# A two-layer hybrid decoder step: ScalarE in program order from the token-major projections to the indexer's end, and the sample tokens' taps as one product and one sum

## The chip, the cores and the metric

The kernel runs on 1 core of a Trainium2 chip. The metric is the device time of one execution in microseconds, the median of several runs.

## The reference, cut to what matters

One inference step over `DEPTH = 2` layers for 1040 prompt tokens (16 meta tokens and 1024) and 64 sample tokens (8 sequences of 8), 1104 columns in all, in float32. Each layer has three branches on one normalised input: a gated linear recurrence, a Conformer convolution and sparse attention whose keys an indexer picks. What the change touches is the gate and the depthwise convolution of the second branch and the projections and scores of the third:

```python
def conformer_conv(glu_in, z, buf, conv_w, conv_b, ln_g, ln_b, conv_pw, w_pb):
    a, g = jnp.split(glu_in, 2, axis=-1)
    u = a * jax.nn.sigmoid(g)
    xp = jnp.concatenate([buf.astype(u.dtype), u], axis=1)
    y = lax.conv_general_dilated(xp, conv_w[:, None, :].astype(xp.dtype), window_strides=(1,), padding='VALID', dimension_numbers=('NWC', 'WIO', 'NWC'), feature_group_count=B_WIDTH) + conv_b
...
def index_scores(qi, wi, ki):
    s = jnp.einsum('bqhd,bsd->bqhs', qi.astype(F32), ki.astype(F32))
    return jnp.einsum('bqhs,bqh->bqs', jax.nn.relu(s), wi.astype(F32) * IDX_SCALE)
```

The convolution has 31 taps and 512 channels (four blocks `c` of 128), the indexer 4 heads of 64.

## The kernel before, in words

**The filler.** The main projections are products of 128 output channels with all 1104 columns. A chunk of 128 channels is worked in three groups of 384, 384 and 336 columns, each 24 matmuls into one PSUM bank `mm` (`stream`, L391): high and low halves of the operands stand apart, so three products make one float32 product. Behind a group's last matmul ScalarE evicts the bank with the bias into `sp` (L204, called behind L391), and behind the third group it issues the DMA that stores the chunk to DRAM (L404). The weights of a chunk are one load `wr`, a cast `wh` on ScalarE in two pieces of 128x512 (L269) and the rest `wl` on GpSimd (L270); the load of the next chunk is asked for ahead of a chunk's first group. This stream is doled out in steps of three matmuls: `fill(key)` takes as many steps as the table `FILL` has under the key, so TensorE always has matmuls between the steps of other work. TensorE's order is the program's order everywhere (`manual_schedule` for that engine); the other engines' orders are a scheduler's, but for VectorE, which keeps program order from the convolution to the masks (the stack `dve`).

**The side work.** The convolution `conv` runs on VectorE: for each of four channel blocks 31 taps over the prompt's 1040 columns (L1492, L1495) and 31 over the 64 sample columns (L1493, L1496). The input `up`, `us` is the projection `ga` times the sigmoid of `gg`; both come back from DRAM, and the sigmoid is one ScalarE operation of 128x1104 for each block (`cy<-cy`). `Side` doles the taps out: each place of the program adds a budget from the table `SIDE` (in ns), each tap pair takes 1420 of it.

**The stretch around the change.** In each layer, one after the other: (1) the first chunks, with budgets `t0`; (2) `cproj`, the token-major projections, two column groups of nine token blocks: weights `cr` are loaded and split into `ch` (ScalarE) and `cl` (GpSimd), each block takes 24 matmuls (L679 to L681) into a bank of `mm` or `tp`, ScalarE copies it to `CTr` (L684), GpSimd adds the bias, and in the second group VectorE rotates it (L722) and takes budget `tr`; (3) `fill("ic")`; (4) `indexer`. It casts the index keys (L733), takes the rest on GpSimd (L734), transposes them (L739) and copies them to `KIH`, `KIL` (L743, L744). Then come the blocks i = 7 to 2 with four heads each: the scores of one head go to the one buffer `lg` (L770, L771; 128(i+1) columns), `fill("is", 7 - i)` takes 6, 4, 7, 6, 7 and 7 steps for i = 7 to 2, ScalarE evicts `lg` through a relu to `rl` (L204, two buffers), and VectorE takes budget `ti` and adds `rl` times a weight to the scores `SC` (L805). The sample tokens' keys (`kir`, `kib`, L888, L893) follow.

Since there is one `lg`, the first score matmul of a head waits until the `rl` of the head before it is done:

```python
for h in range(4):
    ps = lgt()
    ...
    fill("is", 7 - i)
    rl = xt.tile([128, 1152], F32, name="rl", tag="rl")
    act_(rl[:, 0:n], ps[:, 0:n], AF.Relu)
    taps("ti", 7 - i)
```

Of the kernel before, what the change touches and what calls it, by code (L numbers as in the profile page):

```python
# [11 lines left out]
def _quiet(msg, *args, **kwargs):  # L12
# [5 lines left out]
F32 = mybir.dt.float32  # L18
# [31 lines left out]
SIDE = {"t0": (5000, 10000, 10000, 10000, 9300, 10000), "tr": (4200, 4200, 4200, 4200, 4200, 4200, 4200, 2000, 0),  # L50
# [3 lines left out]
KSEL = 4  # L54
# [100 lines left out]
def trunk(tc, a, o, depth=DEPTH):  # L155
# [47 lines left out]
    def act_(out, in_, fn, **kw):  # L203
        S.activation(out, in_, fn, **kw)  # L204
# [136 lines left out]
    def stream(l, pv, chunks, groups, slot, early, lead, more):  # L341


        n = len(chunks)
        blocks = chunks + [("early", (c, bi)) for c in range(8) for bi in range(2)]
        parts = [(c, g) for g in range(3) for c in range(lead)]
        parts += [(i, g) for i in range(lead, n - 2) for g in range(3)]
        parts += [(i, g) for g in range(3) for i in (n - 2, n - 1)]
        parts += [(i, g) for i in range(n, n + 16) for g in range(3)]
        ws, bufs = {}, {}  # L350

        def get(i):
            if i < len(blocks) and i not in ws:
                nm, c = blocks[i]
                if nm == "early":
                    ws[i] = ws[i - 2][1:] if c[0] % 2 else wpair(l, BLK["pb" if c[1] else "pa"] + c[0] // 2)
                else:
                    ws[i] = wchunk(l, BLK[nm] + c, V if i == lead else G, more if 1 < i < lead else None)

        get(0)  # L360
        get(1)
        yield True
        for i, g in parts:
            if g == 0 and 0 < i < lead - 1:
                get(i + 1)
            if lead <= i < n - 1 or i >= n or (i in (lead - 1, n - 1) and g == 2):
                get(i + 1)
            nm, c = blocks[i]
            if nm == "early":
                yield from early.part(c[1], c[0], g, ws[i][0], slot[0])  # L370
                continue
            bcol = BCOL[nm]
            wh, wl = ws[i]
            if g == 0:
                bufs[i] = spt(more if 1 < i < lead else None)
            n0, nn = groups(nm)[g]
            ps = slot[0]()[:, 0:nn]
            sl = slice(n0, n0 + nn)
            H, L = ([x[:, k, sl] for k in range(8)] for x in (XH, XL))
            if i == 0:  # L380

                ops = []
                for k in range(10):
                    if k < 8:
                        ops += [(wh(k), H[k]), (wl(k), H[k])]
                    if k > 1:
                        ops.append((wh(k - 2), L[k - 2]))
            else:
                ops = [(wh(k), x[k]) for k in range(8) for x in (H, L)] + [(wl(k), H[k]) for k in range(8)]
            for j, (w, x) in enumerate(ops):  # L390
                T.matmul(ps, w, x, start=(j == 0), stop=(j == 23))  # L391
                if j == 23:

                    fn = AF.Sigmoid if nm == "gate" and c < 16 else AF.Identity
                    act_(bufs[i][:, sl], ps, fn, bias=pv[:, bcol + c:bcol + c + 1])
                    if nm in ("cz",):

                        if g == 0:
                            sg = spt()
                        act_(sg[:, sl], ps, AF.Sigmoid, bias=pv[:, bcol + c:bcol + c + 1])  # L400
                        G.tensor_tensor(bufs[i][:, sl], bufs[i][:, sl], sg[:, sl], op=OP.mult)
                    if g == 2:
                        lo = groups(nm)[0][0]
                        S.dma_start(fD[nm][c, :, lo:NT], bufs[i][:, lo:NT])  # L404
                    if i == n - 1:
                        early.load(g)
                if j % 3 == 2:
                    yield True
# [164 lines left out]
    def layer(l, hst, late):  # L573
# [39 lines left out]
        slot[0] = mmt  # L613
        ctp = ctr.enter_context(tc.tile_pool(name="ctr", bufs=1, side="right"))
        CTr = ctp.tile([128, 9, 580], F32, name="CTr", tag="CTr")
        cproj(l, CTr, taps)
        scp = scs.enter_context(tc.tile_pool(name="scp", bufs=1))
        SC = scp.tile([128, SCN], F32, name="SC", tag="SC")
        SC8 = scp.tile([128, NT], F32, name="SC8", tag="SC8")
        fill("ic")  # L620
        indexer(l, CTr, SC, SC8, fill, taps)
        ctr.close()
        tk1 = tks.enter_context(tc.tile_pool(name="tk1", bufs=1))
        steps, F = topk(SC, SC8, tk1)
# [30 lines left out]
        return merge(l, pv, late_groups, fill, ers)  # L655


    def cproj(l, CTr, taps):
        with tc.tile_pool(name="cpk", bufs=CPK, side="right") as cpk, tc.tile_pool(name="cpr", bufs=2, side="right") as cpr, \
                tc.tile_pool(name="cpt", bufs=2, side="right") as cpt:  # L660
            for gi, (c0, w) in enumerate(CGROUPS):
                brep = cpr.tile([128, 290], F32, name="brep", tag="brep")
                Y.dma_start(brep[:, 0:w], a["b_in"][l, c0:c0 + w].partition_broadcast(128))
                ch, cl = [], []
                for k2 in range(4):
                    cr = cpr.tile([128, 2, 290], F32, name="cr", tag="cr")
                    Y.dma_start(cr[:, :, 0:w], a["wc"][l, gi, k2])
                    for k in range(2):
                        h_ = cpk.tile([128, 290], F32R, name="ch", tag="ch")
                        l_ = cpk.tile([128, 290], F32R, name="cl", tag="cl")  # L670
                        S.copy(h_[:, 0:w], cr[:, k, 0:w])
                        G.tensor_tensor(l_[:, 0:w], cr[:, k, 0:w], f(h_[:, 0:w]), op=OP.subtract)
                        ch.append(h_)
                        cl.append(l_)
                for t in range(9):
                    rows, ts = TROWS[t], slice(128 * t, 128 * t + TROWS[t])
                    ps = dmt()
                    for k in range(8):
                        T.matmul(ps[0:rows, 0:w], XH[:, k, ts], ch[k][:, 0:w], start=(k == 0), stop=False)  # L679
                        T.matmul(ps[0:rows, 0:w], XH[:, k, ts], cl[k][:, 0:w], start=False, stop=False)  # L680
                        T.matmul(ps[0:rows, 0:w], XL[:, k, ts], ch[k][:, 0:w], start=False, stop=(k == 7))  # L681
                    d0 = c0 - O_C - 512
                    dst = CTr[0:rows, t, d0:d0 + w]
                    S.copy(dst, ps[0:rows, 0:w])  # L684
                    G.tensor_tensor(dst, dst, brep[0:rows, 0:w], op=OP.add)
                    if gi == 1:
                        rope(CTr[0:rows, t, 0:576].rearrange("p (h d) -> p h d", d=64), 9, t, rows, cpt, ((0, 2), (4, 9)))
                        taps("tr", t)
            for dst, j0, j1 in ((kvD.rearrange("t p c -> (t p) c"), 0, 256), (o["kv"][l], 0, 256), (o["ki"][l], 512, 576)):
                Y.dma_start(dst[0:1024].rearrange("(t p) c -> p t c", p=128), CTr[:, 0:8, j0:j1])  # L690
                Y.dma_start(dst[1024:NT], CTr[0:80, 8, j0:j1])
# [772 lines left out]
    def conv(l, pv, cw, c1):  # L1464
        def gated(c):
# [7 lines left out]
            Y.dma_start(y, fD["gg"][c])  # L1473
            Y.dma_start(sr[:, 0], a["state_conv"][l, c])
            G.tensor_copy(us[:, :, 0:30], sr[:, 0])
            act_(y, y, AF.Sigmoid)
            G.tensor_tensor(up[:, 30:1070], up[:, 30:1070], y[:, 0:1040], op=OP.mult)
            G.tensor_tensor(us[:, :, 30:38], us[:, :, 30:38], y[:, 1040:1104].rearrange("p (b q) -> p b q", q=8), op=OP.mult)

# [6 lines left out]
        for c in range(4):  # L1486
            up, us, y = nxt
            yp, ys = y[:, 0:1040], y[:, 1040:1104].rearrange("p (b q) -> p b q", q=8)
            for j in range(31):
                w = cw[:, j, c:c + 1]  # L1490
                if j == 0:
                    V.tensor_scalar(yp, up[:, 0:1040], w, pv[:, 64 + c:65 + c], op0=OP.mult, op1=OP.add)  # L1492
                    V.tensor_scalar(ys, us[:, :, 0:8], w, pv[:, 64 + c:65 + c], op0=OP.mult, op1=OP.add)  # L1493
                else:
                    V.scalar_tensor_tensor(yp, up[:, j:j + 1040], w, yp, op0=OP.mult, op1=OP.add)  # L1495
                    V.scalar_tensor_tensor(ys, us[:, :, j:j + 8], w, ys, op0=OP.mult, op1=OP.add)  # L1496
                if j == 30:
                    Y.dma_start(yD[c], y)
                if j == 14 and c < 3:
                    nxt = gated(c + 1)  # L1500
                yield 1420

    def conv_norm(pv, cn, fill, side):

# [271 lines left out]
```

## Time and profile before

| what | value |
|---|---|
| time, median of 3 runs | 2926.06 us (2922.28 to 2927.58) |
| the profiled execution | 2926.8 us, its span 2924.9 us |
| PE busy | 2757.9 us, 94% of the span |
| DVE busy | 2113.7 us, 72% |
| ACT busy | 1186.8 us, 41% |
| POOL busy | 1247.6 us, 43% |
| chain that ended last | PE 17%, DVE 4%, all others 1% or less |

PE (TensorE) is busy nearly throughout, so the other engines (DVE is VectorE, ACT ScalarE, POOL GpSimd, SP SyncE) matter where PE waits for them. Shares over the whole span hide stages: what a place is worth is read from the waits in its stretch.

### The profile page before, as it was taken

To read this page: it belongs to the slowest core of one execution; us is meant where nothing else is said; L and a number is where in the kernel's file an instruction comes from. 1 tells how busy PE (TensorE), PEld (TensorE's weight loads), DVE (VectorE), ACT (ScalarE), POOL (GpSimd) and SP (SyncE) were. 2 spreads that over 40 slices of the span, in tenths; PEclk is the share of its full clock that TensorE was granted. 3 is DMA by queue.
4 is the path that set the end of the run, shared out by engine and by line. 5 is a ranking of instruction groups with operands and counts; after the bars stand their busy time and mean duration, and the time that the engine had idled before them with its cause. 6 is when DMAs were issued, how large, how long until landed. Compare 5 with 4: busy or idle time off the path is not lost. (4 is left out here: it accounts for less than half of the span.)

```text
span 2924.9 us, 44993 instructions
## 1 busy us (share of the span) xinstructions
PE 2757.9 (94%) x17094; PEld 2620.9 (90%) x17094; DVE 2113.7 (72%) x3832; ACT 1186.8 (41%) x2369; POOL 1247.6 (43%) x978
## 2 busy tenths in 40 slices
PE   7989899999998999999999998998999999999898
PEld 7988879999998888879999997898999989988798
DVE  5798867889969667535366896788899786774443
ACT  4314443323333556544341334422332335565432
POOL 3533334434425214756564332443434241157563
PEclk9999999999999999999999999999999999999999
DMA  4523234332335124666453322323332441247554
GB/s 146 162 61 109 90 103 140 122 112 89 118 130 170 67 67 154 195 201 197 150 169 105 98 83 90 127 99 109 130 112 77 157 151 63 86 150 222 190 166 148
DMA packets 192569, 374.14 MB, mean 128 GB/s; under 512 B 30657, under 2 KB 129697, under 8 KB 192289
## 3 DMA queue, kind: packets, MB, share of 16 engines
q1 hardware_dynamic: 166016, 272.21, 29.7%
q10 hardware_dynamic: 20448, 78.09, 6.6%
q0 software_dynamic: 5888, 20.97, 2.3%
q8 instruction: 134, 2.20, 0.3%
q14 instruction: 83, 0.67, 0.1%
HBM read 251.07 MB, written 122.40 MB: 128 GB/s over the span
## 5 line engine op out<-in xcount | busy, mean ns | idle before, releaser
L391 PE MATMUL mm<-xh,wh 128*128 128x384 f32 (+2 forms) x2656 | 888.1, 336 | 27.6 <-ACT sp L204 23.9
L391 PE MATMUL mm<-xl,wh 128*128 128x384 f32 (+2 forms) x2656 | 886.0, 336 | 0.0
L270 POOL TENSOR_TENSOR wl<-wr,wh 128x512 fp32r<-128x512 f32 x332 | 473.1, 1443 | 697.8 <-ACT wh L269 465.8
L391 PEld LDWEIGHTS mm<-xh,wh 128*128 128x128 f32 x2656 | 506.0, 191 | 41.5 <-ACT sp L204 29.0
L391 PE MATMUL mm<-xh,wl 128*128 128x384 f32 (+2 forms) x2656 | 531.3, 336 | 0.0
L391 PEld LDWEIGHTS mm<-xl,wh 128*128 128x128 f32 x2656 | 506.2, 191 | 7.2 <-issue 1.9
L391 PEld LDWEIGHTS mm<-xh,wl 128*128 128x128 f32 x2656 | 461.8, 192 | 6.3 <-issue 1.9
L916 DVE TENSOR_SCALAR_CACHE_REDUCE jk<-SC,F 80x1104 bf16<-80x1104 f32 (+6 forms) x448 | 448.8, 1002 | 8.4
L204 ACT ACTIVATE sp<-mm,vec 128x384 f32<-128x384 f32 (+1 forms) x356 | 198.6, 564 | 512.0 <-PE mm L391 494.8
L1495 DVE SCALAR_TENSOR_TENSOR cy<-up,vec,cy 128x1040 f32<-128x1040 f32 x240 | 337.9, 1408 | 0.4
L269 ACT CAST wh<-wr 128x512 fp32r<-128x512 f32 x352 | 203.6, 618 | 164.1 <-PE mm L391 80.4
L204 ACT ACTIVATE P<-P,nm 128x896 f32<-128x896 f32 (+7 forms) x128 | 99.5, 778 | 64.1 <-DVE nm L1021 61.7
L1037 DVE TENSOR_TENSOR pl<-tp,ph 128x512 fp32r<-128x512 f32 x144 | 97.8, 687 | 36.9 <-ACT ph L1036 36.1
L1496 DVE SCALAR_TENSOR_TENSOR cy<-us,vec,cy 128x64 f32<-128x64 f32 x240 | 117.2, 488 | 0.0
L1036 ACT CAST ph<-tp 128x512 fp32r<-128x512 f32 x144 | 83.2, 584 | 54.4 <-PE tp L1033 50.2
L1021 DVE CUSTOM_DVE_ANT_0 P<-sc,MB 128x512 f32<-128x512 f32 (+1 forms) x96 | 63.9, 667 | 57.1 <-PE sc L1015 56.2
L1346 PEld LDWEIGHTS lg<-hQ,hK 128*128 128x128 f32 x512 | 65.8, 205 | 28.0 <-issue 19.9
L1025 DVE TENSOR_SCALAR P<-P,nm 128x896 f32<-128x896 f32 (+7 forms) x128 | 87.4, 683 | 4.3
L1346 PE MATMUL lg<-hQ,hK 128*128 128x64 f32 x512 | 66.4, 286 | 25.5 <-DVE hQ L1375 25.3
L1033 PE MATMUL tp<-ident,P 128*128 128x128 f32 x576 | 88.0, 275 | 1.5 <-DVE P L1025 1.5
L204 ACT ACTIVATE rl<-lg 128x1024 f32<-128x1024 f32 (+6 forms) x54 | 42.6, 788 | 102.8 <-DVE SC L805 60.2
L287 PE MATMUL tp<-xh,wh 128*128 128x384 f32 (+2 forms) x240 | 79.9, 335 | 0.4 <-DVE z L1681 0.4
(454 smaller groups left out, 5932.0 us busy)
## 6 DMA issues: line engine op xcount, KB each, us to landing
wr<-in_wp SPq DMA_DIRECT2D x180, 512.0 KB
eg<-gateD SPq DMA_DIRECT2D x80, 184.0 KB
gateD<-sp ACTq DMA_DIRECT2D x24, 552.0 KB
gateD<-sp ACTq DMA_DIRECT2D x24, 544.0 KB
cr<-in_wc SPq DMA_DIRECT2D x16, 290.0 KB
gt<-gateD SPq DMA_DIRECT2D x24, 192.0 KB
za<-zaD SPq DMA_DIRECT2D x24, 192.0 KB
ggD<-sp ACTq DMA_DIRECT2D x8, 552.0 KB
```

The lines of the kernel that those rows point to most:

```text
L204: S.activation(out, in_, fn, **kw)
L269: S.copy(wh[:, k:k + 4], wr[:, k:k + 4])
L270: (eng or G).tensor_tensor(wl[:, k:k + 4], wr[:, k:k + 4], f(wh[:, k:k + 4]), op=OP.subtract)
L391: T.matmul(ps, w, x, start=(j == 0), stop=(j == 23))
L916: V.tensor_scalar(jk[0:rows, 0:n], s, F.bitcast(F32)[0:rows, j:j + 1], None, op0=OP.is_ge, op1=OP.add, accum_out=cnt[0:rows, j:j + 1])
L1025: V.tensor_scalar(p[:, 0:n], p[:, 0:n], nm[:, 3:4], None, op0=OP.mult)
L1033: T.transpose(ps[:, 128 * c:128 * c + 128], P[c][:, 128 * kt:128 * kt + 128], ident)
L1036: S.copy(ph, ps)
L1037: V.tensor_tensor(pl, ps, f(ph), op=OP.subtract)
L1346: T.matmul(ps[:, 64 * c:64 * c + 64], K[:, 128 * c:128 * c + 128], up(Q[:, 128 * c:128 * c + 128], m), start=True, stop=True)
L1495: V.scalar_tensor_tensor(yp, up[:, j:j + 1040], w, yp, op0=OP.mult, op1=OP.add)
L1496: V.scalar_tensor_tensor(ys, us[:, :, j:j + 8], w, ys, op0=OP.mult, op1=OP.add)
```

## The change

Four edits, the first three of order and of arithmetic, the last of the two budgets:

1. `cproj` first loads and splits the weights of both column groups, then enters ScalarE into program order; `act.close()` ends that behind the indexer. So ScalarE's order there is now the order in which the program is written.
2. The sigmoid of `gg` for blocks c = 2 and 3 is taken in the eviction of the projection; blocks 0 and 1 keep the operation of their own.
3. The 31 sample taps of a block become, four times, one product of 128x496 (two sequences x 8 tokens x 31 taps) and one sum over the taps; then one addition of the bias. The product tile takes the buffer of `sr` (tag `sr`, one buffer). A prompt tap is priced 1200, a product with its sum 1300.
4. `SIDE`: `tr` goes from 4200 to 3200 (2000 to 1000), `ts` from 3000 to 4000.

```diff
-SIDE = {"t0": (5000, 10000, 10000, 10000, 9300, 10000), "tr": (4200, 4200, 4200, 4200, 4200, 4200, 4200, 2000, 0),
-        "tk": 4200, "ti": (1400, 2800, 2800, 2800, 2800, 2800), "ts": 3000,
+SIDE = {"t0": (5000, 10000, 10000, 10000, 9300, 10000), "tr": (3200, 3200, 3200, 3200, 3200, 3200, 3200, 1000, 0),
+        "tk": 4200, "ti": (1400, 2800, 2800, 2800, 2800, 2800), "ts": 4000,
...
-                    fn = AF.Sigmoid if nm == "gate" and c < 16 else AF.Identity
+                    fn = AF.Sigmoid if (nm == "gate" and c < 16) or (nm == "gg" and c >= 2) else AF.Identity
...
-        cproj(l, CTr, taps)
+        act = ExitStack()
+        cproj(l, CTr, taps, act)
...
         indexer(l, CTr, SC, SC8, fill, taps)
+        act.close()
...
+                groups.append((gi, c0, w, brep, ch, cl))
+
+            act.enter_context(tc.manual_schedule(engines={mybir.EngineType.Activation}))
+            for gi, c0, w, brep, ch, cl in groups:
                 for t in range(9):
...
-            act_(y, y, AF.Sigmoid)
+            if c < 2:
+                act_(y, y, AF.Sigmoid)
...
-                    V.tensor_scalar(ys, us[:, :, 0:8], w, pv[:, 64 + c:65 + c], op0=OP.mult, op1=OP.add)
                 else:
                     V.scalar_tensor_tensor(yp, up[:, j:j + 1040], w, yp, op0=OP.mult, op1=OP.add)
-                    V.scalar_tensor_tensor(ys, us[:, :, j:j + 8], w, ys, op0=OP.mult, op1=OP.add)
+                if j < 4:
+
+                    b2 = us[:, 2 * j:2 * j + 2, 0:8]
+                    pr = c1.tile([128, 2, 8, 31], F32, name="spr", tag="sr")
+                    V.tensor_tensor(pr, bass.AP(b2.tensor, b2.offset, [*b2.ap, [1, 31]]),
+                                    cw[:, :, c].unsqueeze(1).unsqueeze(1).to_broadcast([128, 2, 8, 31]), op=OP.mult)
+                    V.tensor_reduce(ys[:, 2 * j:2 * j + 2], pr, AX.X, OP.add)
+                    yield 1300
+                if j == 4:
+                    V.tensor_scalar(ys, ys, pv[:, 64 + c:65 + c], None, op0=OP.add)
...
-                yield 1420
+                yield 1200
```

TensorE's order is the same in both programs, instruction for instruction. ScalarE's is not; three places follow.

ScalarE in layer 0, in `cproj`, the program before: copies of token blocks to `CTr` (blocks 4 and 5 around the sigmoid of channel block 2).

```order
L684 COPY CTr_1210<-tp_1343 128x290
L684 COPY CTr_1210<-tp_1370 128x290
L204 ACTIVATE cy_1665<-cy_1665 128x1104
L684 COPY CTr_1210<-tp_1397 128x290
L684 COPY CTr_1210<-mm_1424 128x290
```

In the changed program the copies (L691 there) stand one behind the other; there is no sigmoid of that kind for blocks 2 and 3.

ScalarE in layer 0, from the last `CTr` copy to the cast of the index keys, before:

```order
L684 COPY CTr_1210<-mm_1879 80x290
L204 ACTIVATE sp_1935<-mm_1936,vec_107 128x384
L204 ACTIVATE sp_1935<-mm_1962,vec_107 128x384
L733 CAST rl_2069<-CTr_1210 128x8x64
L269 CAST wh_2016<-wr_2015 128x512 x2
L204 ACTIVATE sp_1935<-mm_1988,vec_107 128x336
L404 DMA vD_92<-sp_1935 128x1104
L733 CAST rl_2069<-CTr_1210 80x64
```

and in the changed program:

```order
L691 COPY CTr_1195<-mm_1841 80x290
L269 CAST wh_1890<-wr_1889 128x512 x2
L204 ACTIVATE sp_1897<-mm_1898,vec_107 128x384
L204 ACTIVATE sp_1897<-mm_1924,vec_107 128x384
L204 ACTIVATE sp_1897<-mm_1950,vec_107 128x336
L404 DMA vD_92<-sp_1897 128x1104
L269 CAST wh_1978<-wr_1977 128x512 x2
L204 ACTIVATE sp_1985<-mm_1986,vec_107 128x384
L740 CAST rl_2031<-CTr_1195 128x8x64
```

The cast of the keys, which stood ahead of the third group's eviction, now stands behind it, its DMA, the next weights and the next chunk's first eviction.

ScalarE in the indexer of layer 0, the four heads of block 7, before (`rl` reads a head's scores `lg`, `sp` evicts a filler group):

```order
L204 ACTIVATE rl_2227<-lg_2202 128x1024
L204 ACTIVATE sp_2188<-mm_2189,vec_107 128x384
L204 ACTIVATE rl_2264<-lg_2232 128x1024
L762 CAST qs_2240<-tp_2237 64x2x128
L763 CAST qs_2240<-tp_2237 64x2x128
L204 ACTIVATE cy_2496<-cy_2496 128x1104
L204 ACTIVATE sp_2188<-mm_2220,vec_107 128x384
L204 ACTIVATE rl_2293<-lg_2269 128x1024
L269 CAST wh_2312<-wr_2311 128x512 x2
L204 ACTIVATE rl_2333<-lg_2298 128x1024
L204 ACTIVATE sp_2188<-mm_2274,vec_107 128x336
L404 DMA aqD_90<-sp_2188 128x1104
```

and in the changed program, the same heads:

```order
L204 ACTIVATE sp_2146<-mm_2147,vec_107 128x384
L204 ACTIVATE rl_2185<-lg_2160 128x1024
L769 CAST qs_2197<-tp_2194 64x2x128
L770 CAST qs_2197<-tp_2194 64x2x128
L204 ACTIVATE sp_2146<-mm_2178,vec_107 128x384
L204 ACTIVATE rl_2221<-lg_2189 128x1024
L204 ACTIVATE rl_2250<-lg_2226 128x1024
L204 ACTIVATE sp_2146<-mm_2231,vec_107 128x336
L404 DMA aqD_90<-sp_2146 128x1104
L269 CAST wh_2271<-wr_2270 128x512 x2
L204 ACTIVATE rl_2292<-lg_2257 128x1024
```

Where a filler group ends in a head's fill, its `sp` (and behind a 336 group the DMA and mostly the next `wh`) now stands ahead of that head's `rl`; before, `rl` stood ahead of it.

## Rows read from the trace of the kernel before

**Rows 1.** PE, waits in 60:347 us, layer 0: releaser, total, times, longest (us)

```profile
PE tp L679 <- ACT CTr L684: 6.2, 1, 6.2
PE mm L391 <- ACT sp L204: 6.0, 2, 4.3
PE lg L770 <- ACT rl L204: 4.1, 4, 1.6
PE tp L777 <- ACT KIL L744: 1.7, 1, 1.7
PE lg L770 <- DVE qs L764: 0.7, 1, 0.7
```

**Rows 2.** Timeline of ACT, 143:167 us: start, length, instruction, [idle before <-releaser]

```profile
165.09 1.12 ACT L204 ACTIVATE cy<-cy 128x1104 f32<-128x1104 f32 x1 [20.48 <-DMA cy<-ggD]
```

**Rows 3.** Stretches: each engine's busy us (x), granted PE clock, DMA share, GB/s

```profile
166.50:171.10 4.60, 4.54 (x19) 4.54 (x20) 3.88 (x4) 1.19 (x5) 4.54 (x5) 0.51 0.02 3
215.10:219.30 4.20, 4.12 (x18) 4.03 (x18) 4.20 (x6) 0.03 (x1) 3.65 (x3) 0.59 1.03 347
231.60:327.00 95.40, 89.64 (x515) 85.46 (x516) 91.96 (x123) 39.02 (x74) 30.88 (x20) 1.00 0.26 86
1662.00:1666.20 4.20, 4.12 (x19) 4.12 (x20) 4.17 (x7) 2.52 (x6) 1.24 (x2) 0.59 0.49 77
```

**Rows 4.** PE, waits in 1500:1765 us, layer 1; the `lg` row in 60:1765, both layers

```profile
PE mm L391 <- ACT sp L204: 2.1, 2, 1.7
PE mm L679 <- ACT sp L204: 3.2, 1, 3.2
PE tp L777 <- ACT KIL L744: 2.0, 1, 2.0
PE tp L739 <- POOL rl L734: 1.0, 1, 1.0
...
PE lg L770 <- ACT rl L204: 8.2, 8, 1.6
```

**Rows 5.** Timeline of ACT, 231:262 us, the first indexer heads of layer 0

```profile
234.91 0.58 ACT L204 ACTIVATE sp<-mm,vec 128x384 f32<-128x384 f32 x1 [1.06 <-PE mm L391]
...
240.77 0.58 ACT L204 ACTIVATE sp<-mm,vec 128x384 f32<-128x384 f32 x1
241.25 1.02 ACT L204 ACTIVATE rl<-lg 128x1024 f32<-128x1024 f32 x1
243.66 1.14 ACT L269 CAST wh<-wr 128x512 fp32r<-128x512 f32 x2 [1.39 <-PE mm L391]
...
245.87 0.53 ACT L204 ACTIVATE sp<-mm,vec 128x336 f32<-128x336 f32 x1
246.44 0.33 ACTq L404 DMA_DIRECT2D aqD<-sp  x1
...
259.90 0.92 ACT L204 ACTIVATE rl<-lg 128x896 f32<-128x896 f32 x1 [2.47 <-DVE SC L805]
```

**Rows 6.** Timeline of PE, 232:236 and 260.5:262 us, in the same heads

```profile
233.32 1.55 PE L391 MATMUL mm<-xh,wl 128*128 128x384 f32 x8
234.71 0.34 PE L391 MATMUL mm<-xh,wh 128*128 128x384 f32 x1
...
260.87 0.50 PE L770 MATMUL lg<-KIH,qs 128*128 128x512 f32 x1 [1.40 <-ACT rl L204]
261.21 0.39 PE L771 MATMUL lg<-KIL,qs 128*128 128x512 f32 x1
```

**Rows 7.** Groups of 231:327 us by shape: busy us, mean ns, idle before

```profile
L204 ACT ACTIVATE rl<-lg 128x768 f32<-128x768 f32 x4 | 3.2, 812 | 7.8 <-DVE SC L805 5.5 <-DVE SC L803 2.2
...
L204 ACT ACTIVATE rl<-lg 128x384 f32<-128x384 f32 x3 | 1.5, 486 | 6.0 <-DVE SC L805 6.0
```

**Rows 8.** Timeline of POOL, 205:222 us: the split of the index keys in layer 0

```profile
213.73 1.55 POOL L734 TENSOR_TENSOR rl<-CTr,rl 128x512 f32<-128x512 f32 x1 [14.55 <-ACT rl L733]
```

**Rows 9.** The page's groups, whole program: the sample tokens' taps

```profile
L1496 DVE SCALAR_TENSOR_TENSOR cy<-us,vec,cy 128x64 f32<-128x64 f32 x240 | 117.2, 488 | 0.0
```

More of the change, by code (lines that the diff above doesn't have):

```diff
@@ L655, in layer, with cproj @@
         return merge(l, pv, late_groups, fill, ers)
-    def cproj(l, CTr, taps):
+    def cproj(l, CTr, taps, act):
         with tc.tile_pool(name="cpk", bufs=CPK, side="right") as cpk, tc.tile_pool(name="cpr", bufs=2, side="right") as cpr, \
                 tc.tile_pool(name="cpt", bufs=2, side="right") as cpt:
+            groups = []
             for gi, (c0, w) in enumerate(CGROUPS):
```

## The prediction

> **What bounds the kernel now.** The table of engines says it first: PE is busy 94% of the span, so a microsecond is won or lost where PE waits. I therefore read the list of PE's waits, stretch by stretch, and then the engine named as releaser on its own timeline.
>
> In layer 0, from 60 to 347 us, PE waits for ScalarE in four places that the change touches [rows 1]: 6.2 us for a copy to `CTr`, 6.0 in two waits for a filler eviction (4.3 and 1.7), 4.1 in four waits for `rl`, 1.7 for the last key copy; and 0.7 for VectorE's `qs`. The first has a plain cause: ScalarE stood 20.48 us in front of the sigmoid of channel block 2, waiting for its input's DMA, with finished banks queued behind it [rows 2]. Each long wait costs twice, since PE then runs at the lower of its two clocks (1.2 instead of 2.4 GHz) for a while. The granted clock was 0.51 over the 4.6 us behind the 6.2 us wait and 0.59 over the 4.2 us behind the 4.3 us wait [rows 3]: 4.6 x 0.49 = 2.25 and 4.2 x 0.41 = 1.72 us lost. Layer 1 shows the same places with 2.1, 3.2, 2.0 and 1.0 us and for `rl` another 4.1, half of both layers' 8.2 [rows 4], and 0.59 for 4.2 us behind the 2.0 us wait, 1.72 lost [rows 3].
>
> In the indexer's heads PE is busy 89.64 of 95.40 us at clock 1.00 [rows 3]: only 5.8 us could be gained there. VectorE, busy 91.96, is nearly full, yet PE waits just 4.1 us for what VectorE holds up.
>
> **Removed.** The sigmoids of blocks 2 and 3 as operations, hence the 6.2 us and its clock; the eviction queued behind the keys' cast, hence 4.3 and its clock; the eviction wait of 1.7 at the heads' end; all four `rl` waits (they come back below, from another cause); `qs` 0.7; of the key copies' 1.7 all but 0.4, which I leave for the twelve copies themselves. Layer 0: 6.2 + 6.0 + 4.1 + 1.3 + 0.7 = 18.3, plus clocks 2.25 + 1.72 = 4.0, together 22.3 us. Layer 1: 2.1 + 4.1 + 3.2 + 1.6 + 1.0 = 12.0, plus 1.7, together 13.7. Sum 36.0 us.
>
> **Added: a wait in most heads.** PE's order is unchanged, so which filler group ends in which head's fill is fixed and can be counted. In program order `rl` stands behind the eviction of such a group, while the next head's first matmul needs `rl` done. The time from the group's last matmul to that point is a sum of rows. The eviction starts 0.20 us after the matmul that follows the group (234.91 against 234.71) [rows 5, 6]. ScalarE goes on 0.48 us after a 384 eviction starts (240.77 to 241.25), 0.57 after a 336 one; then 0.36 for the chunk's DMA issue (0.33 in the row) and 1.03 for a pair of `wh` (1.14 long, overlapping the next) [rows 5]. `rl` takes 1.02 at 1024 columns [rows 5], 0.92 at 896 [rows 5], 0.81 at 768 and 0.49 at 384 [rows 7]; 640 and 512 lie between, 0.70 and 0.60. PE starts 0.05 after it (259.90 + 0.92 = 260.82 to 260.87) [rows 5, 6]. Against this stands the head's remaining fill: (234.71 - 233.32) / 8 = 0.175 us per matmul of 384 [rows 6], 0.153 at 336.
>
> Worked out, with what is left of the fill in brackets:
> - block 7: head 0, 0.20 + 0.48 + 1.03 + 0.05 - 1.05 (6 matmuls) = 0.71; head 1, nothing left, 1.76; head 3, 336 group with DMA and `wh`, 3.24 - 2.10 = 1.15
> - block 6: heads 0 and 2, nothing left, 1.65 each
> - block 5: 1.44, 0.49, 1.08 and, a 336 group with the DMA but `wh` behind, 0.20 + 0.57 + 0.36 + 0.81 + 0.05 = 1.99
> - block 4: 0.51 and 1.88; block 3: 0.71; block 2: 0.30 and, three matmuls left, 0.20 + 0.57 + 0.36 + 1.03 + 0.49 + 0.05 - 0.52 = 2.18
>
> Fourteen waits, 17.5 us per layer, the same in both. VectorE does not lengthen them: budget `ti` is unchanged and buys less work than before.
>
> **Added elsewhere.** The keys' cast now stands behind the third group's eviction, a `wh` pair and the next eviction. In layer 1 the last of these ends three filler steps before the transposes: 0.20 + 0.48, the cast at about 0.6 (the 384 eviction's length [rows 5]), GpSimd's rest at 1.55 [rows 8], two hand-overs of 0.05, less 9 x 0.175: 1.4 us. In layer 0 VectorE's rotations may be later still: between 1.4 and 4.3, the wait that this place had [rows 1]; I take 2.3, near the low end, as `tr` gives VectorE less to do there. The sample keys' copies stand behind one more `wh` pair: 1.1 per layer [rows 5]. Sum of new waits: 2 x 17.5 + 1.4 + 2.3 + 2 x 1.1 = 40.9 us. A wait also costs its restart, about 0.1 us (the first matmul behind one lasts 0.50, the next 0.39 [rows 6]); there are some 14 more waits than before: 1.4.
>
> **Clock of the new waits.** No drop shows behind the waits of up to 1.6 in the heads (clock 1.00), a drop behind 2.0 [rows 1, 3, 4]. I take a drop behind the two longest of each layer, 1.99 and 2.18, at 1.7 each: 6.8 us; the ends are none and one behind each of the six waits over 1.6 per layer, 20.4 us.
>
> The Trainium skill ("TensorE: Matmul & The Clock Gate", section "A second HAM failure mode: psum-queue depth-cycling") says that frequent short idles between matmul groups can by themselves make the clock swing between its two levels; by that rule the sum would take the upper end, 20.4 in place of 6.8. The trace speaks against it so far: the heads already had short waits at clock 1.00 [rows 3].
>
> **Off the path.** The 240 small taps took 117.2 us of VectorE, 0.488 each [rows 9]. In their place come 32 products, 32 sums and 8 additions; between 0.49 and 1.55 each (the small tap, GpSimd's 512-column operation [rows 8, 9]), 35 to 112 us: VectorE gains 5 to 82 us, I take about 70, as for operations that VectorE does alone. It is worth 0 to PE, whose waits for VectorE here are the 0.7 already counted; it shortens only the lag behind `SC`. Its first product waits for the store that frees the `sr` buffer, ahead of which VectorE merely takes longer for block 0. The second column group's weight splits moved ahead of the first group's copies cost 0 as long as the filler's weights of those chunks are there in time; if not, up to 6.2, the longest wait here [rows 1], which the range includes.
>
> **The sum.** New 40.9 + 1.4 + 6.8 = 49.1, removed 36.0: 13.1 us slower. The profiled execution took 2926.8 (span 2924.9 and 1.9 around it), 0.7 above the median: 2926.8 + 13.1 - 0.7 = 2939.2 us against 2926.1.
>
> **The rivals.** A measurement of this kernel can tell about 0.2% (5.9 us) from no change.
> - *The waits come, the clock holds.* Each head's wait stays below what drops the clock. For it: clock 1.00 behind waits of 1.4 to 1.6 [rows 3, 6]. 2926.1 + 4.9 + 1.4 = 2932.4, at the edge of no change.
> - *The eviction costs a head nothing, so the change is faster.* If the group's eviction lies wholly beside PE's last fill matmuls, each wait loses 0.20 + 0.48 + 0.05 = 0.73: nine long ones lose 6.6 and the five short ones vanish, 2.7, so 18.6 over both layers. 2932.4 - 18.6 = 2913.8. It decides where ScalarE gets to `rl` less than 0.1 us behind the group's end. Against it: the lag of 0.20 and the step of 0.48 are read from rows [rows 5, 6].
> - *The clock drops behind every wait above 1.6.* 2932.4 + 20.4 = 2952.8. For it: they follow one another within 4 to 8 us, closer than before.
> - *It does nothing on balance.* ScalarE's new order gives back as much as it takes, and the products take as long as the small taps: 2926.
>
> **How the numbers follow.** Forecast 0.38, clock holds 0.24 (0.14 of it within 0.2%), eviction hidden 0.20, clock drops everywhere 0.12, nothing 0.06. So faster 0.20, same 0.14 + 0.06 = 0.20, slower 0.38 + 0.10 + 0.12 = 0.60. As both signs hold weight, the range reaches from the hidden-eviction case to the all-drops case, 2913 to 2953; the forecast's own range is 2932 to 2946 (no drop, four more drops).
>
> **What would show it.** In the profile after: no `cy` sigmoid of 20 us idle and no 6.2 us wait in `cproj`; in the heads some 14 waits of `lg` for `rl` with 17 us in each layer, the longest about 2.2 in block 2, with `rl` directly behind `sp` on ScalarE; a granted clock below 1.00 in the heads; VectorE's total down by tens of us. Wrong would be `lg` waits below 9 us per layer (evictions hidden), VectorE as the releaser of them, or a PE wait in the first chunks for weights.

## The result, and the profile after

The changed kernel takes 2950.68 us (median of 4, 2944.35 to 2952.47) beside 2924.86 for the kernel before in the same comparison: ratio 1.0083, 95% interval 1.0068 to 1.0098. It is 25.8 us slower, inside the range of 2913 to 2953, with the sign that was forecast; the forecast's own 13.1 us was half of it, and the time lies outside the forecast's own range of 2932 to 2946.

The span was cut at the first matmuls of three places, all starts read from PE's timeline: `cproj`, the first head, the first transposition of the sample keys (`kir`), in both layers.

| stretch, us | before | after | difference | in the prediction |
|---|---|---|---|---|
| start to `cproj`, layer 0 | 127.8 | 128.6 | +0.8 | 0 |
| `cproj` to the first head, layer 0 | 103.75 | 102.91 | -0.8 | -14.2 |
| heads, layer 0 | 105.63 | 117.38 | +11.8 | +11.7 and 3.4 for the clock |
| `kir` of layer 0 to `cproj` of layer 1 | 1235.3 | 1239.0 | +3.7 | +1.1 |
| `cproj` to the first head, layer 1 | 95.54 | 88.11 | -7.4 | -6.5 |
| heads, layer 1 | 105.55 | 118.98 | +13.4 | +11.7 and 3.4 for the clock |
| the rest | 1151.3 | 1155.8 | +4.5 | +1.1 |

(The prediction's 1.4 us of restarts lie over all rows.) So the heads came as worked out, layer 1 too, and layer 0's stretch ahead of the heads gave nothing.

PE's waits in the changed kernel, 60 to 348 us (layer 0) and then 1570 to 1790 us (layer 1); columns as in [rows 1]:

```profile
PE lg L777 <- ACT rl L204: 15.3, 13, 2.1
PE tp L746 <- POOL rl L741: 14.1, 1, 14.1
```

```profile
PE tp L746 <- POOL rl L741: 1.0, 1, 1.0
PE tp L784 <- ACT KIL L751: 0.4, 1, 0.4
```

All waits of [rows 1] but that for `rl` are gone in layer 0. In their place stand 15.3 us for `rl` in 13 waits, and one of 14.1 us for the index keys' rest on GpSimd (layer 1 shows the same 15.3 and 13, and 1.0). Who is late for that one shows on ScalarE's timeline and on VectorE's:

```profile
203.23 0.58 ACT L204 ACTIVATE sp<-mm,vec 128x384 f32<-128x384 f32 x1 [2.04 <-PE mm L391]
216.52 0.62 ACT L740 CAST rl<-CTr 128x512 fp32r<-128x512 f32 x1 [12.71 <-DVE CTr L729]
```

```profile
175.58 0.79 DVE L725 TENSOR_TENSOR rA<-CTr,cb 128x144 f32<-128x144 f32 x1 [2.93 <-POOL CTr L692]
...
206.81 3.97 DVE L1502 SCALAR_TENSOR_TENSOR cy<-up,vec,cy 128x1040 f32<-128x1040 f32 x3
...
216.09 0.34 DVE L729 TENSOR_TENSOR CTr<-rA,rB 128x32 f32<-128x32 f32 x2
```

ScalarE had evicted the filler's group at 203.23, as the program order says, and then stood 12.71 us for VectorE's rotation of the eighth token block, whose last operation began at 216.09. Behind the cast comes GpSimd's rest, which before began at 213.73 [rows 8]; GpSimd's timeline now:

```profile
217.22 1.55 POOL L741 TENSOR_TENSOR rl<-CTr,rl 128x512 f32<-128x512 f32 x1 [13.86 <-ACT rl L740]
```

So VectorE got there 3.5 us later, not earlier, and TensorE, freed of the waits ahead, arrived at 204.8 (218.82 less 14.06) and waited.

The timelines show two things behind VectorE's lateness. The DMA that ScalarE's sigmoid had waited for [rows 2] now holds up GpSimd's product for `up`, with the bias additions and so the first rotation behind it. And since program order puts the casts `wh` ahead of the keys' cast, GpSimd's two splits `wl` now lie among the rotations (at 189.03 and 200.74 us; before, the first began at 215.25, behind them). Beside them VectorE's pair of operations L729, 0.34 us in most other blocks, lasted 4.17 and 2.47 us. GpSimd's and VectorE's timelines of the changed kernel:

```profile
164.52 2.03 POOL L1485 TENSOR_TENSOR up<-up,cy 128x1040 f32<-128x1040 f32 x1 [5.46 <-DMA cy<-ggD]
```

```profile
187.62 4.17 DVE L729 TENSOR_TENSOR CTr<-rA,rB 128x32 f32<-128x32 f32 x2
```

```profile
189.03 2.55 POOL L270 TENSOR_TENSOR wl<-wr,wh 128x512 fp32r<-128x512 f32 x2
```

The heads, PE's timeline in layer 0: the first head waits after the change, against the list in the prediction (0.71, 1.76, 1.15 in block 7; 1.65 and 1.65 in block 6; 1.44 in block 5):

```profile
236.27 0.50 PE L777 MATMUL lg<-KIH,qs 128*128 128x512 f32 x1 [0.54 <-ACT rl L204]
...
242.44 0.50 PE L777 MATMUL lg<-KIH,qs 128*128 128x512 f32 x1 [1.58 <-ACT rl L204]
...
251.38 0.50 PE L777 MATMUL lg<-KIH,qs 128*128 128x512 f32 x1 [1.01 <-ACT rl L204]
...
256.03 0.50 PE L777 MATMUL lg<-KIH,qs 128*128 128x512 f32 x1 [1.48 <-ACT rl L204]
...
263.81 0.50 PE L777 MATMUL lg<-KIH,qs 128*128 128x512 f32 x1 [1.48 <-ACT rl L204]
...
272.21 0.50 PE L777 MATMUL lg<-KIH,qs 128*128 128x512 f32 x1 [1.35 <-ACT rl L204]
```

Each is 0.1 to 0.2 us shorter than worked out, and at its place. The stretches of the heads show a clock of 1.00 and 0.99 (columns as in [rows 3]; the first row is the 14 us wait, the second what follows it, at 0.52; the last two are what follows the longest wait of the heads, 2.09 us, in layer 0 and in layer 1):

```profile
204.70:218.80 14.10, 0.06 (x1) 0.00 (x0) 13.85 (x24) 0.62 (x1) 1.55 (x1) 0.57 0.11 39
218.80:224.00 5.20, 5.17 (x20) 5.08 (x21) 0.76 (x5) 4.18 (x8) 0.32 (x1) 0.52 0.95 316
231.50:348.88 117.38, 101.94 (x576) 95.35 (x576) 107.33 (x107) 40.97 (x81) 35.99 (x25) 1.00 0.24 85
1675.95:1794.93 118.98, 103.54 (x576) 96.93 (x576) 107.87 (x113) 40.98 (x81) 36.67 (x25) 0.99 0.24 84
338.20:343.00 4.80, 4.72 (x27) 4.72 (x28) 4.67 (x4) 0.42 (x2) 2.04 (x2) 1.00 0.35 117
1782.70:1787.00 4.30, 4.29 (x16) 4.29 (x17) 4.26 (x3) 0.00 (x0) 1.96 (x2) 0.61 0.29 88
```

So the same wait left the clock at 1.00 in layer 0 and was followed by 0.61 over 4.3 us in layer 1: 4.3 x 0.39 = 1.7 us, about the 1.6 us by which layer 1's heads are the longer ones.

### The profile page after: what moved, and what is told of

Read it like the earlier page. It is cut to its first block, busy times and chain, and to the rows that moved or that the text cites. A ratio compares the mean times of both kernels' runs of the same rounds, so it can differ in the third digit from the quotient of the medians.

```text
span 2950.7 us, 44803 instructions
## 1 busy us (share of the span) xinstructions
PE 2759.6 (94%) x17094; PEld 2618.0 (89%) x17094; DVE 2125.1 (72%) x3656; ACT 1185.2 (40%) x2365; POOL 1257.7 (43%) x978
## 5 line engine op out<-in xcount | busy, mean ns | idle before, releaser
L1502 DVE SCALAR_TENSOR_TENSOR cy<-up,vec,cy 128x1040 f32<-128x1040 f32 x240 | 356.1, 1484 | 5.8
L287 PE MATMUL tp<-xl,wh 128*128 128x384 f32 (+2 forms) x240 | 78.7, 330 | 0.0
L1040 PEld LDWEIGHTS tp<-ident,P 128*128 128x128 f32 x576 | 70.2, 140 | 7.0 <-DVE P L1032 1.9
```

Of the source, the lines that this page charges most:

```text
L287: T.matmul(ps[:, 0:nn], wk, x, start=(n == 0), stop=(n == 3 * K - 1))
L1040: T.transpose(ps[:, 128 * c:128 * c + 128], P[c][:, 128 * kt:128 * kt + 128], ident)
```

## The experiments

All twelve, with the stretches of their profiled executions (ahead of the heads in layer 0, heads, ahead of the heads in layer 1, heads; us). The ratio is to the kernel before in the same comparison; it need not be the quotient of the two medians.

| run | median us | ratio (95%) | layer 0 ahead | heads | layer 1 ahead | heads |
|---|---|---|---|---|---|---|
| before | 2924.9 | 1 | 103.8 | 105.6 | 95.5 | 105.6 |
| the change | 2950.7 | 1.0083 (1.0068, 1.0098) | 102.9 | 117.4 | 88.1 | 119.0 |
| e1_rl_first | 2925.8 | 1.0007 (0.9994, 1.0020) | 102.5 | 106.3 | 88.1 | 106.3 |
| e2_tr_low | 2965.7 | 1.0148 (1.0127, 1.0169) | 89.2 | 117.6 | 89.2 | 120.6 |
| e4_sched_order | 2938.1 | 1.0043 (1.0023, 1.0064) | 108.3 | 111.9 | 91.1 | 111.8 |
| e5_sigmoid_only | 2917.0 | 0.9984 (0.9970, 0.9997) | 104.4 | 105.6 | 92.1 | 104.4 |
| e6_products_only | 2943.1 | 1.0070 (1.0044, 1.0096) | 109.9 | 109.2 | 99.9 | 108.2 |
| e7_rl_first_taps_later | 2915.4 | 0.9969 (0.9958, 0.9981) | 89.2 | 106.4 | 89.2 | 106.5 |
| e8_split_only | 2925.9 | 1.0006 (0.9992, 1.0020) | 104.5 | 105.6 | 99.2 | 105.7 |
| e9_sigmoid_taps_later | 2916.7 | 0.9976 (0.9961, 0.9991) | 102.8 | 106.5 | 90.9 | 106.5 |
| e10_small_taps_best | 2904.3 | 0.9926 (0.9911, 0.9941) | 92.7 | 102.6 | 88.1 | 101.7 |
| e11_products_old_price | 2934.8 | 1.0028 (1.0013, 1.0043) | 111.8 | 109.7 | 96.5 | 108.8 |
| e12_close_early | 2916.3 | 0.9964 (0.9952, 0.9975) | 89.2 | 110.7 | 89.2 | 110.9 |
| e13_no_edit3 | 2951.1 | 1.0087 (1.0061, 1.0114) | 102.4 | 117.3 | 92.7 | 117.3 |

**The heads: `rl` ahead of the filler.**

```diff
-                    fill("is", 7 - i)
                     rl = xt.tile([128, 1152], F32, name="rl", tag="rl")
                     act_(rl[:, 0:n], ps[:, 0:n], AF.Relu)
+                    fill("is", 7 - i)
```

> The changed kernel with one edit: in the indexer's heads the relu `rl` is written ahead of the filler call instead of behind it; TensorE's order is the same. Theory A (the eviction that stands ahead of `rl` makes the heads' waits): the waits of `lg` for `rl`, 30.6 us in 26 over both layers in the changed kernel, fall to about the 8 us of before, and the time by 20 to 24 us, to about 2928. Theory B (VectorE sets the pace of the heads through the two `rl` buffers): the waits stay above 20 us with VectorE's `SC` as what ScalarE waits for, and the time moves by less than 8 us.

2925.8 us: two lines exchanged took back 24.9 us by the medians, 22 by the ratios. The heads fell from 117.4 and 119.0 to 106.3, their waits in layer 0 from 15.3 to 4.9 us. PE's waits in 60 to 338 us of this run, and the longest of what ScalarE waits for in 231 to 337 us, in the heads, first of this run, then of the change:

```profile
PE tp L746 <- POOL rl L741: 13.9, 1, 13.9
PE lg L777 <- ACT rl L204: 4.9, 3, 2.3
```

```profile
ACT rl L204 <- DVE SC L812: 25.9, 11, 4.7
```

```profile
ACT sp L204 <- PE mm L391: 52.1, 17, 4.3
```

With `rl` behind the filler ScalarE stood 52 us for the filler's matmuls in front of `sp`, with a finished `lg` queued behind; with `rl` first it waits for VectorE's `SC` instead, as before the change [rows 7]. Theory A. The 13.9 us wait for the keys stayed and cost nothing against before, since the whole stretch is as long as before (102.5 against 103.8).

**Layer 0 ahead of the heads: who is late.** Three runs bear on it. The first gives VectorE fewer taps between the rotations:

```diff
-SIDE = {"t0": (5000, 10000, 10000, 10000, 9300, 10000), "tr": (3200, 3200, 3200, 3200, 3200, 3200, 3200, 1000, 0),
+SIDE = {"t0": (5000, 10000, 10000, 10000, 9300, 10000), "tr": (1200, 1200, 1200, 1200, 1200, 1200, 1200, 0, 0),
...
```

> The changed kernel with the budget `tr` at 1200 instead of 3200 for each token block (0 instead of 1000 for the eighth): 12 prompt taps of 1.3 us, some 15 us of VectorE, move from between layer 0's rotations to places behind. Theory A (VectorE's chain of rotations and taps sets layer 0's 14.1 us wait for the index keys): the wait falls to 3 us or less, the clock behind it stays at 1.00, and the time falls by 10 to 14 us, to about 2938. Theory B (ScalarE's new order or GpSimd's bias additions set it): the wait stays above 10 us and the time stays. Theory C (the taps moved are late for the convolution's norm): the wait falls but the time stays within 5 us, with a new wait of PE behind the heads.

PE's waits, 60 to 260 and then 345 to 480 us of this run:

```profile
PE tp L746 <- POOL rl L741: 1.0, 1, 1.0
```

```profile
PE tp L1532 <- POOL nsq L1529: 13.6, 1, 13.6
```

The wait for the keys fell from 14.1 to 1.0 and the stretch from 102.9 to 89.2: VectorE's rotations and taps set it, theory A for the place. The time rose by 15 us, for theory C's reason but by more than its 5: the taps moved were left over behind the indexer and came back as 13.6 us at the convolution's norm in each layer. Layer 1, where nothing was to gain, lost them whole.

The second puts the sigmoid alone into the kernel before (edit 2):

> The kernel before with edit 2 alone: the sigmoid of blocks 2 and 3 in the projection's eviction. Theory A (VectorE's chain of rotations is the bound of layer 0's stretch, and the 6.2 us wait for the copy only lay ahead of it): the 6.2 us wait and the 20.5 us of ScalarE go, a wait for the eviction or for the index keys takes their place, the first head of layer 0 starts within 2 us of 231.6, and the time falls by 2 to 6 us (layer 1's 3.2 us and little more), to about 2921. Theory B (each removed wait is gain, as the prediction had it): the first head of layer 0 starts 8 us earlier, the time falls by 11 us or more, to 2914 or less.

2917.0 us, 7.1 us faster by the medians and 4.7 by the ratio (0.9 to 8.8): nearer to theory A. The 6.2 us wait is gone, and this stands in its place (PE's waits, 60 to 260 us, and ScalarE's timeline there):

```profile
PE mm L391 <- ACT sp L204: 13.4, 1, 13.4
```

```profile
210.23 0.62 ACT L733 CAST rl<-CTr 128x512 fp32r<-128x512 f32 x1 [18.48 <-DVE CTr L722]
...
217.01 0.24 ACT L733 CAST rl<-CTr 80x64 fp32r<-80x64 f32 x1 [4.68 <-DVE CTr L722]
```

The 13.4 us are longer than the 6.2 and 4.3 of before together; ScalarE's cast of the keys, which the scheduler put ahead of the eviction, waits for VectorE. The stretch is 104.4 us long, 103.8 before: taking the sigmoid's wait away gave layer 0 nothing. What the run gained lies in layer 1 (4.6 us in its two stretches) and outside the stretches of the table.

The third does both, in the kernel before: the sigmoid in the eviction, `tr` 2800 in place of 4200, `ts` 4500 in place of 3000.

> The kernel before with the sigmoid in the eviction and some 8 tap pairs moved out of layer 0's and 1's rotations: `tr` 2800 in place of 4200 (1400 for the eighth), `ts` 4500 in place of 3000. Theory A (behind the 6.2 us wait stood VectorE's chain): the 13.4 us wait for the eviction that the sigmoid alone leaves falls to 3 us or less, time 2903 to 2909. Theory B (something else holds the keys' cast, GpSimd or ScalarE's order): the wait stays above 8 us, time 2915 or more.

2916.7 us and a wait of 14.1 us for `sp`: theory B. VectorE was done with the eighth block's rotation at 204.5 there, but the scheduler had put both casts of the keys ahead of two filler evictions, and the second waits for the ninth block. So the two halves need each other: program order for ScalarE, and a shorter chain on VectorE.

**Both, with the moved taps where VectorE stands idle.** The change with `rl` first, `tr` 1200, and `ts` 6000:

> The changed kernel with `rl` ahead of the filler, `tr` at 1200 and `ts` raised from 4000 to 6000, so that the 12 taps moved out of the rotations run where VectorE stood idle for 14.9 and 11.9 us (its waits for the sample scores). Theory A (VectorE's chain makes the 14 us wait of layer 0, and the 13.6 us wait at the convolution's norm came from taps left over behind the indexer): both waits go, time 2910 to 2916, below both kernels. Theory B (the taps moved cost wherever they stand): a wait of over 8 us at the norm stays, time 2925 or more.

2915.4 us, 8.3 below the kernel before, theory A. Both waits are gone (keys 1.0 us, norm 3.7 as in the kernel before), and layer 0's stretch takes 89.2 us as layer 1's does.

**The products.** Edit 3 alone in the kernel before:

> The kernel before with edit 3 alone: products and sums for the sample taps with their prices 1300 and 1200; the budgets, ScalarE's order and the sigmoid are those of before. Theory A (VectorE's share is off TensorE's path, as the prediction had it): VectorE busy 50 to 90 us less, time within 6 us of 2924. Theory B (the cheaper prices put more taps of 1.3 us into each budget, 2800 / 1200 in place of 2800 / 1420, and so make the rotations and the heads later): VectorE's total falls by less than 30 us, layer 0's rotations end some 8 us later and the heads wait more for `rl`, time 2935 to 2945.

2943.1 us, theory B: 19 us slower, all four stretches longer (by 6.1, 3.6, 4.3 and 2.7). VectorE's busy time went from 2113.7 to 2110.7 us, in the change to 2125.1. The groups of the changed kernel, and two places where VectorE works alone, first before, then after:

```profile
L1502 DVE SCALAR_TENSOR_TENSOR cy<-up,vec,cy 128x1040 f32<-128x1040 f32 x240 | 356.1, 1484 | 5.8
L1507 DVE TENSOR_TENSOR spr<-us,vec 128x496 f32<-128x496 f32 x32 | 46.1, 1441 | 5.5 <-DMA out_s_conv<-sr 5.5
L1509 DVE TENSOR_REDUCE cy<-spr 128x16 f32<-128x496 f32 x32 | 21.5, 671 | 1.1
```

```profile
140.22 1.29 DVE L1495 SCALAR_TENSOR_TENSOR cy<-up,vec,cy 128x1040 f32<-128x1040 f32 x1
141.43 0.28 DVE L1496 SCALAR_TENSOR_TENSOR cy<-us,vec,cy 128x64 f32<-128x64 f32 x1
141.62 1.29 DVE L1495 SCALAR_TENSOR_TENSOR cy<-up,vec,cy 128x1040 f32<-128x1040 f32 x1
```

```profile
206.81 3.97 DVE L1502 SCALAR_TENSOR_TENSOR cy<-up,vec,cy 128x1040 f32<-128x1040 f32 x3
```

A tap pair goes by in 141.62 - 140.22 = 1.40 us although its halves last 1.29 and 0.28. Taps one behind another, each reading what the one ahead wrote, follow at (3.97 - 1.29) / 2 = 1.34. So where VectorE is alone a small tap costs 0.06 us, 2 us a block, and not the 0.488 of [rows 9]. What replaced it, in the changed kernel where VectorE is alone too:

```profile
161.88 1.29 DVE L1502 SCALAR_TENSOR_TENSOR cy<-up,vec,cy 128x1040 f32<-128x1040 f32 x1
163.09 1.05 DVE L1507 TENSOR_TENSOR spr<-us,vec 128x496 f32<-128x496 f32 x1
164.18 0.67 DVE L1509 TENSOR_REDUCE cy<-spr 128x16 f32<-128x496 f32 x1
164.77 2.87 DVE L1502 SCALAR_TENSOR_TENSOR cy<-up,vec,cy 128x1040 f32<-128x1040 f32 x1
```

A product with its sum costs 164.77 - 161.88 - 1.34 = 1.55 us there, 6.2 a block. These are prices for VectorE alone; over the whole program its busy time moved by only -3.0 us (this run) and +11.4 (the change), so the gain of about 70 is not there, and no loss of 4 us a block either. And a tap of 1.34 us was now priced 1200 where a pair of 1.40 had been priced 1420, so each budget held more time than before. The same run with the old price, its edit against this one:

```diff
-                    yield 1300
+                    yield 0
...
-                yield 1200
+                yield 1420
```

> The kernel before with edit 3 alone, as in the run that gave 2943.1, but a prompt tap priced 1420 as a pair was and a product with its sum 0, so that each place takes the taps that it took before. Theory A (the price of 1200 for a tap of 1.34 us made the run 19 us slower, more taps in each place): layer 0's wait for the keys falls from 18.2 to near what the kernel before shows, layer 1's 6.0 to near 1, time 2924 to 2932. Theory B (the products and sums themselves do it): the waits stay within 4 us of 18.2 and 6.0, time 2938 or more.

2934.8 us, between the theories: of the 19 us some 11 went with the price (ratios 1.0070 and 1.0028) and 8 stayed with the products. Layer 1's wait of 6.0 us went; in layer 0 a wait of 14.2 us for `sp` took the place of the 18.2 for the keys. Its profiled execution took 2949.3, so its stretches are above its median; that split is a rough one. And the change with edits 3 and 4 undone:

> The changed kernel with edits 3 and 4 undone: small sample taps, their price of 1420 and the budgets of before; ScalarE's program order, the split loops and the sigmoid in the eviction stay, and `rl` stays behind the filler. Theory A (the heads' waits make the loss, the products add to it through VectorE): the waits for `rl` stay near 30 us over both layers, layer 0's wait for the keys is 8 to 14 us, time 2936 to 2944, some 10 us below the changed kernel. Theory B (the products cost nothing in this setting, since layer 0's rotations are late either way): within 4 us of 2950. Theory C (without the products each removed wait is gain, as the prediction's sum had it): layer 0's wait for the keys is 4 us or less and the time 2932 or less.

The change without edits 3 and 4 takes 2951.1 us, as long as the change itself: theory B. With the smaller `tr` beside them the products neither added nor took anything there, and the wait for the keys stood at 13.4 us with the old taps too (PE's waits, 60 to 260 us):

```profile
PE tp L746 <- POOL rl L741: 13.4, 1, 13.4
PE lg L777 <- ACT rl L204: 4.6, 4, 1.6
```

**The order alone, the split alone, the end of the order.** The scheduler's order in the changed kernel:

> The changed kernel without its program order on ScalarE (the call that enters it is taken out; the loops stay split, the sigmoid in the eviction and the products stay): the scheduler orders ScalarE again. Theory A (the program order is what costs): the heads' waits for `rl` fall from 30.6 to about 8 us, layer 0's wait for the index keys stays near 14 us since VectorE and GpSimd set it, the time is 2925 to 2932. Theory B (the products or the moved weight splits cost): the time stays above 2945.

2938.1 us, between the theories: 13 us of the 25.8 go. The heads wait less but still take 112 us, and a wait of 18.5 us for `sp` takes the place of that for the keys: in the scheduler's order both casts again stand ahead of the eviction.

The split of the loops alone, in the kernel before:

> The kernel before with the loops of the token-major projections split alone: both column groups' weights are loaded and split first, the scheduler still orders ScalarE. Theory A (it costs nothing, as the prediction had it): 2920 to 2928. Theory B (the loads and splits moved up hold up the filler's weights, GpSimd's bias additions or the first channel block): 2932 or more, with a PE wait in the first 230 us that the kernel before has not.

2925.9 us: no cost of the split shows (the interval reaches from -2 to +6 us), theory A.

ScalarE's program order ended earlier:

> The changed kernel with `rl` ahead of the filler and the taps moved, as in the run that gave 2915.4, with ScalarE's program order ended behind the heads instead of behind the sample keys. Theory A (the weights' casts ahead of the copies to `kib` cost 1 us per layer): the waits for `kib`, 6.4 us in four, fall to the 4.5 of before, time 2911 to 2915. Theory B (the scheduler puts other work ahead there): the time does not fall, with new waits of PE between the heads' end and the norm.

2916.3 us beside 2915.4: theory B. The waits for `kib` fell to 4.5 us, but a wait of 3.1 us for `sp` came in each layer, and the heads' stretches went to 110.7 and 110.9.

**The version that beats both.** The change with `rl` first, taps moved, and the small taps kept:

> The changed kernel with `rl` ahead of the filler and the taps moved behind the rotations as in the run before (2915.4 us), but with edit 3 undone: small sample taps again at 1420 a pair, `tr` 2800 (1400 for the eighth), `ts` 4500. Theory A (the products cost VectorE more than the small taps: alone, a tap pair goes by in 1.40 us, taps one behind another in 1.34, and four products with their sums need 6.5 us a block): VectorE's total is lower than with products, layer 0's keys wait 1 us or less, time 2905 to 2914. Theory B (the products save VectorE time once the budgets fit): 2917 to 2926, with more waits for `rl`.

2904.3 us, ratio 0.9926 (0.9911 to 0.9941): 22 us below the kernel before, 46 below the change. PE's waits in 60 to 324 us:

```profile
PE tp L746 <- POOL rl L741: 4.5, 1, 4.5
PE lg L777 <- ACT rl L204: 3.1, 5, 0.9
```

The time is theory A's, the reason only in part. VectorE was busy for 2116.1 us, not less than the 2112.9 of the run that gave 2915.4, and the wait for the keys is 4.5 us where 1 was expected. The heads took 102.6 and 101.7 us in place of 106.4 and 106.5 (in layer 0 ScalarE waited 39.3 us for VectorE's `SC`, 44.8 there), and the stretch from `kir` of layer 0 to `cproj` of layer 1 took 1232.3 in place of 1241.8. The price of a tap went back to 1420 with the small taps, so each head's budget of 2800 also holds fewer of them: how much of the 11 us is the products' and how much the price's, this run does not separate.

## Why the prediction was right in sign and half in size

- **The heads: right.** Fourteen waits and 17.5 us a layer were forecast, 13 and 15.3 measured, in the places and nearly the lengths of the list; e1 shows that the order of `rl` and `sp` makes them. Removing the old waits there was counted rightly as well: +11.7 forecast, +11.8 and +13.4 measured, the second with 1.7 of a clock drop in it.
- **Layer 1 ahead of the heads: right.** -6.5 forecast, -7.4 measured; its wait for the keys 1.4 forecast, 1.0 measured.
- **Layer 0 ahead of the heads: the step that failed.** "hence the 6.2 us and its clock; the eviction queued behind the keys' cast, hence 4.3 and its clock" was taken as gain, with 2.3 us for the wait that comes next, bounded by 4.3 as "the wait that this place had". It measured 14.1. The bound was wrong in kind: the old wait was short because TensorE had been held up 6.2 us before, and lost time at the low clock. Taken away, these come back whole in the wait behind, if the engine that it waits for is no earlier. So they did: ahead of layer 0's heads, waits and low clock took 6.2 + 4.3 + 1.7 + 0.7 + 4.0 = 16.9 us before and 14.1 + 5.2 x 0.48 = 16.6 after. VectorE was not earlier: its smaller budget of 3200 still held three taps of 1.34 us in most blocks, its first rotation began at 175.58, behind GpSimd, and it lost some 6 us beside GpSimd's splits. The last is a cost of edit 1 that the prediction did not see: from the first rotation to the last operation of the eighth passed 4.5 us more in e13 (with program order) than in e5 (without), at the same taps, budgets and sigmoid (43.3 and 38.8 us). That it is GpSimd's split that lengthens VectorE's operations is read from the two timelines and not shown by a run of its own. e5, e2 and e7 show from three sides that VectorE's chain sets the stretch: without the sigmoid's wait the stretch stays at 104 us, with a shorter chain on VectorE it falls to 89. This step alone is 13.4 us; the forecast missed 12.7 in all, and the other misses nearly cancel.
- **The clock of the new waits: wrong.** 6.8 us were set for a drop behind the two longest of each layer's waits; one came, behind layer 1's 2.09 us, worth 1.7. The rival with a drop behind every wait above 1.6 falls: there were six such waits. The rule of the Trainium skill ("TensorE: Matmul & The Clock Gate", section "A second HAM failure mode: psum-queue depth-cycling"), by which frequent short idles can make the clock swing, does not describe these heads: thirteen in 117 us left it at 1.00 in layer 0, and in layer 1 it fell once.
- **VectorE off the path: wrong.** "VectorE gains 5 to 82 us, I take about 70", worth 0: its busy time rose by 11.4 us, and e6 shows that what it does is worth 19 us where the budgets are those of before (8 of them with the old price). That the change's own budgets made this up (e13) was not foreseen either; the 0 in the sum was right by accident.
- **The rest: 8.2 us at other places against 2.2 forecast** (+3.7 and +4.5). Part has a name in PE's waits over the whole span (for `kib` from 4.5 to 6.4 us, as forecast; for the norm's `nsq` at its first sum from 1.4 to 3.9; for `bzt` of a later stage from 5.4 to 8.4); the rest is spread over small waits of the later stages and was not followed.
- **The time inside the range: luck.** The range's upper end, 2953, was reached for with a clock drop behind every wait above 1.6 us. The time came near it by another way, through layer 0's stretch ahead of the heads, where the prediction allowed for a wait of at most 4.3 us.

## What to carry to other kernels

Before a wait is counted as gain, ask when the next thing that the engine needs is ready, by its own chain, and count the smaller of the two; an old wait is no bound for a new one behind it. Program order for an engine is only as good as the program text: a result that the next step waits for belongs ahead of work that can wait, and two exchanged lines were worth 22 to 25 us here. What program order moves up on one engine also moves what hangs on it: here GpSimd's splits, into the middle of VectorE's chain. Budgets that dole out work by a price are tied to the true durations, so a cheaper-looking form needs its prices measured where it runs.

## What the runs showed of the hardware

Where VectorE was alone, taps that each read what the one ahead wrote followed at 1.34 us; with an independent tap of 0.28 us between each two they followed at 1.40. The product over 496 columns, read through overlapping windows, lasted 1.05 us at its shortest (second row below), 1.44 in the mean, and 2.30 in the first row, while GpSimd's product for `up` ran (from 98.06 for 2.03 us); VectorE's timeline of the changed kernel:

```profile
98.71 2.30 DVE L1507 TENSOR_TENSOR spr<-us,vec 128x496 f32<-128x496 f32 x1 [3.34 <-DMA out_s_conv<-sr]
...
160.21 1.05 DVE L1507 TENSOR_TENSOR spr<-us,vec 128x496 f32<-128x496 f32 x1
```

And the granted clock stayed at its upper level through thirteen waits of 0.3 to 2.1 us in layer 0's heads, 15.3 us in all; in layer 1 the same thirteen were followed by one drop, 0.61 over 4.3 us behind the 2.09 us wait, as a 2.0 us wait had dropped it in the kernel before [rows 3, 4].
